# First norm of a two-layer DiT trunk: sums of squares on TensorE tile by tile, the first two adaLN tiles moved ahead, and a one-operation first guess of the root

## The chip, the cores and the metric

One core of a Trainium2 chip runs the whole program. The metric is device microseconds of that core, from the first to the last instruction and what lies around them; lower is better. Five engines work beside each other: TensorE (PE: matmuls, and PEld: its weight loads), VectorE (DVE), ScalarE (ACT), GpSimd (POOL) and SyncE (SP, which here issues most transfers).

## The reference, cut to what matters

Two layers of a backbone; what the change touches is the very first norm, and every reciprocal root in the program. D is 1024, the 256 latent and 256 context tokens are handled together as 512 columns.

```python
def rmsnorm(x, g):
    xf = x.astype(jnp.float32)
    y = xf * lax.rsqrt(jnp.mean(xf * xf, axis=-1, keepdims=True) + EPS)
    return y.astype(x.dtype) * g

mod_x = jnp.split((jax.nn.silu(c) @ p['w_ada'] + p['b_ada'])[:, None, :], 6, axis=-1)   # shift, scale, ...
hx = modulate(rmsnorm(xs, p['norm1_g']), mod_x[0], mod_x[1])     # h * (1 + scale) + shift
u = hx @ p['w_in']                                               # then four mixers, a merge, a SwiGLU
```

## The kernel before

Activations lie with channels on the 128 partitions and tokens along the free axis, so x is eight tiles `xs[k]` of 128 channels by 512 tokens. A product is taken as three matmuls on halves of a split operand (`mm3`: high by high, high by low, low by high). Weights arrive in chunks of eight 128-column blocks (`w_load`, a transfer by SP into `raw`) and are split by `w_ensure` into `whi` (a cast on ACT) and `wlo` (two subtractions on DVE).

The program starts with one serial stage, and then a loop over the eight tiles of channels:

- **Sums of squares.** `sq_add` squares each x tile on ACT as it lands and adds it on DVE into an accumulator, so that two tiles are left. `rstd_of(..., False)` calls `tok_sums` (line 469), which multiplies them by a column of ones: for each block of 128 tokens and each of the two tiles one matmul whose stationary side is the 128 by 128 piece of squares and whose moving side is one column. These are 8 matmuls; in float32 each runs as two passes, and the trace shows 16 pairs of weight load and matmul.
- **The root.** `rsqrt` (line 461) takes an integer first guess in two DVE operations (a shift into `rs_i`, then a multiply and add into `rs_y`) and improves it in seven more, each on 128 by 4 numbers, each waiting for the one before. The function serves all 17 roots of the program.
- **The broadcast.** `bcast` puts the root on all partitions with four PE transposes.
- **adaLN of one tile of channels.** `first_mod(u)` multiplies the conditioning vector by the columns of the modulation weights of tile u (16 small matmuls `mx<-u,cs`, 32 passes in the trace), copies the result on ACT, turns it with one matmul by `halves` (`mx<-cons,u`, 128x4), and makes shift and scale on DVE (`mod`, `moda`). Its weights are four transfers of 256 KB, put into SP's queue by `first_load(u)`.
- **The loop.** For each tile u, `norm_apply` makes the modulated tile in both halves (DVE `u<-u,moda,mx`, ACT, DVE), `first_mod(u + 1)` is called, and then 18 matmuls of 512 columns go into six accumulators (`pre`), followed by `first_load(u + 3)`.

Each engine works its own instructions in order. Their order is set by a scheduler that goes by dependences and by priorities from the place in the code, and `tc.high_priority()` lifts the root and the modulation's last operations.

Of the kernel before, what the change touches and what calls it, by code (L numbers as in the profile page):

```python
# [13 lines left out]
I32 = mybir.dt.int32  # L14
AF = mybir.ActivationFunctionType
ALU = mybir.AluOpType
AX = mybir.AxisListType

D = 1024
KD = D // 128  # L20
SEQ = 256
T = 512
L = 2
GRID_W = 64
EPS = 1e-6
# [115 lines left out]
def trunk(ctx: ExitStack, tc: tile.TileContext, xin: bass.AP, cin: bass.AP, par: bass.AP, con: bass.AP,  # L141
# [47 lines left out]
    U = Slots(upool, NSLOT)  # L189
# [4 lines left out]
    def nm(s):  # L194
        cnt[0] += 1
        return f"{s}_{cnt[0]}"
# [4 lines left out]
    def mx():  # L201
        return psx.tile([128, 512], F32, tag="mx", name=nm("mx"))

    def sm(shape, tag, dtype=F32, bufs=2):
        return small.tile(shape, dtype, tag=tag, name=nm(tag), bufs=bufs)

    def width(o):
        n_ = 1
        for d_ in o.shape[1:]:
            n_ *= d_  # L210
        return n_

    def stt(o, i0, s, i1, op0, op1):
        clk["dve"] += 65 + 1.17 * width(o)
        V.scalar_tensor_tensor(out=o, in0=i0, scalar=s, in1=i1, op0=op0, op1=op1)  # L215

    def tt(o, i0, i1, op):
        clk["dve"] += 65 + 1.1 * width(o)
        V.tensor_tensor(out=o, in0=i0, in1=i1, op=op)  # L219

    def red(o, i, op):
        clk["dve"] += 65 + 1.15 * width(i)
        V.tensor_reduce(out=o, in_=i, axis=AX.X, op=op)

    def ts(o, i0, s1, op0, s2=None, op1=None):
        clk["dve"] += 65 + 0.8 * width(o)
        if op1 is None:
            V.tensor_scalar(out=o, in0=i0, scalar1=s1, scalar2=None, op0=op0)
        else:
            V.tensor_scalar(out=o, in0=i0, scalar1=s1, scalar2=s2, op0=op0, op1=op1)  # L230

    MUL, ADD, SUB, MAX = ALU.mult, ALU.add, ALU.subtract, ALU.max
# [58 lines left out]
    xs = []  # L291
    for k in range(KD):
        t = U([128, T])
# [14 lines left out]
    for l in range(L):  # L308
        t = cpool.tile([128, NPAR], F32, name=f"par{l}")
# [3 lines left out]
    one = cpool.tile([128, 1], F32, name="one")  # L313
# [146 lines left out]

    def rsqrt(v, shape):

        y, s, ti = sm(shape, "rs_y"), sm(shape, "rs_s"), sm(shape, "rs_i", I32)
        with tc.high_priority():
            ts(ti, v.bitcast(I32), 1, ALU.logical_shift_right)
            ts(y.bitcast(I32), ti, -1, MUL, 0x5F3759DF, ADD)

            tt(s, y, y, MUL)
            tt(s, s, v, MUL)
            stt(s, s, -10.0 / 3, s, ADD, MUL)  # L470
            stt(y, s, 5.0, y, ADD, MUL)
            stt(s, y, -0.5 * 0.375 ** 3, y, MUL, MUL)
            tt(s, s, v, MUL)
            stt(y, s, 1.5 * 0.375, y, ADD, MUL)
        return y
# [12 lines left out]
    def rstd_of(sums, N, n, merge=True):  # L488
        shape = [128, len(sums), N // 128]
        if merge:  # L490
            r = sm(shape, "toks")
            for i, tiles in enumerate(sums):
                if len(tiles) == 2:
                    t = tiles.pop()
                    tt(tiles[0][:, :N], tiles[0][:, :N], t[:, :N], ADD)
                    U.put(t)
                p = mx()
                for b in range(N // 128):
                    PE.transpose(p[:, b * 128:(b + 1) * 128], tiles[0][:, b * 128:(b + 1) * 128], ident)
                red(r[:, i, :], p[:, :N].rearrange("p (b t) -> p b t", t=128), ADD)  # L500
            ts(r, r, 1.0 / n, MUL, EPS, ADD)
            return rsqrt(r, shape)
        r = sm(shape, "toks")
        ts(r, tok_sums(sums, N), 1.0 / n, MUL, EPS, ADD)
        return rsqrt(r, shape)

    def bcast(r, N):

        p = mx()
        for b in range(N // 128):  # L510
            PE.transpose(p[:, b * 128:(b + 1) * 128], r[:, b:b + 1].to_broadcast([128, 128]), ident)
        return p

    def sq_add(acc, src, N):

        t = U([128, N])
        A.activation(t[:, :N], src, AF.Square)
        acc = acc or []
        if len(acc) < 2:
            return acc + [t]  # L520
        tt(acc[0][:, :N], acc[0][:, :N], acc[1][:, :N], ADD)
        U.put(acc[1])
        return [acc[0], t]
# [71 lines left out]
    def first_load(u):  # L595
        if u < KD:
            ada_tiles[u] = [U([128, 512]) for _ in range(4)]
            for i_, t_ in enumerate(ada_tiles[u]):
                nc.sync.dma_start(t_, wfirst[u, i_])
# [3 lines left out]
    def first_mod(u):  # L603

        p = mx()
        for k in range(KD):
            for h in range(2):
                j = h + 2 * (k % 2)
                PE.matmul(p[32 * j:32 * j + 32, 0:128], cs[:, k, :],
                          ada_tiles[u][k // 2][:, (2 * (k % 2) + h) * 128:(2 * (k % 2) + h + 1) * 128], start=k < 2,  # L610
                          stop=k >= KD - 2, tile_position=(0, 32 * j), skip_group_check=True)
        U.put(ada_tiles.pop(u))
        sb = U([128, 128])
        A.copy(sb, p[:, 0:128])
        PE.matmul(p[:, 128:132], sb, halves, start=True, stop=True, skip_group_check=True)
        U.put(sb)
        o = PCOL["bada"][0]
        with tc.high_priority():
            tt(mods[0][:, u:u + 9:8, :], p[:, 128:132].rearrange("p (h s) -> p h s", h=2),
               params[0][:, o + u:o + u + 9:8].unsqueeze(2).to_broadcast([128, 2, 2]), ADD)  # L620
            stt(moda[:, u, :], mods[0][:, 8 + u, :], 1.0,
                params[0][:, PCOL["n1g"][0] + u:PCOL["n1g"][0] + u + 1].to_broadcast([128, 2]), ADD, MUL)
# [3 lines left out]
    first_load(1)  # L626
    w_load(1)
    first_load(2)
    nc.sync.dma_start(cons[:, nfirst:], con[:, nfirst:nres])
    acc = None  # L630
    for k in range(KD):
        acc = sq_add(acc, xs[k], T)
    rs = rstd_of([acc], T, D, False)
    U.put(acc)
    rb = bcast(rs[:, 0, :], T)
    hx = [None] * KD
    pre = [mm() for _ in range(4)] + [mx() for _ in range(2)]
    pos = w_take([(("w_in", 0), k, cols) for k in range(KD)
                  for cols in [misc_cols] + [ar(OFF["xbc"] + 128 * c) for c in FIRST]])
    W["ahead"], W["load"] = 0, 1  # L640
    began = clk["pe"]
    first_mod(0)
    for u in range(KD):
        hx[u] = U.pair(T)
        for s in range(2):
            norm_apply(hx, xs, s, rb, (moda, mods[0][:, 0:8, :]), u, s * SEQ)
        if u + 1 < KD:
            first_mod(u + 1)
        for i, ps in enumerate(pre):
            wh, wl = w_block(pos + 6 * u + i)  # L650
            mm3(ps, wh, wl, hx[u][0], hx[u][1], u == 0, u == KD - 1)
        first_load(u + 3)
    W["ahead"], W["load"] = AHEAD, NLOAD
    U.put(xs)
    for c0 in range(2048, 6144, 1024):
# [2 lines left out]
    for l in range(L):  # L658
# [643 lines left out]
        xs = []  # L1302
        for k in range(KD):
            t = U([128, N])
# [39 lines left out]
        for a, b in grp:  # L1344
# [28 lines left out]
            else:  # L1373
# [3 lines left out]
                r = out_by_stream(("w_ffn_out", l), act, b - a, a, 40, None if last else (l + 1, "n1g", 0))  # L1377
            U.put(act)
        if last:
            acc = r  # L1380
# [7 lines left out]
    rs = rstd_of([acc], SEQ, D, False)  # L1388
# [3 lines left out]
    for b in range(2):  # L1392
        for h in range(2):
            p, y = mm(), U([128, 512])
# [132 lines left out]
```

## Time and profile before

| | us |
|---|---|
| median of 3 runs | 1694.93 (1694.31 to 1698.3) |
| the profiled execution, as timed | 1695.51 |
| its span, first to last instruction | 1693.8 |
| PE busy in the span | 1649.6 (97%) |
| first 512-column matmul of the loop starts at | 24.84 |
| PE busy ahead of that, of 24.84 | 8.95 |

The page of the profile gives busy times, a row of 40 slices of the span and the chain of work that ended last. The timeline gives instructions in order of time, equal ones merged: start, time taken (of a merged row from its first start to its last end), engine, line, operation, and in brackets the engine's idle time before it and what ended that. PE's matmuls overlap, so how fast a stream of them goes is read from start to start and not from one matmul's own time.

### The profile page before, as it was taken

The page shows a single profiled execution, that of the slowest core. Times are in us where ns is not written, and L with a number is a line of the kernel's source. Part 1 is how long each engine was busy: PE and PEld are TensorE (multiplying, and loading weights), DVE is VectorE, ACT ScalarE, POOL GpSimd, SP SyncE. Part 2 cuts the span into 40 slices and gives each one's busy share as a digit, 9 for nine tenths or more (in the row PEclk, how much of TensorE's full clock was granted, in tenths as well). Part 3 has the DMA queues.
Part 4 walks back from the last instruction along what each step waited for, and adds up shares of the span by engine and source line. Part 5 has one row for each costly group of instructions (what it writes and reads, how often), then busy time and mean ns, then how long its engine had stood idle before and what let it go on. Part 6 is the DMA issues. An engine that isn't in the chain of part 4 may idle for free.

```text
span 1693.8 us, 26526 instructions
## 1 busy us (share of the span) xinstructions
PE 1649.6 (97%) x10078; PEld 1419.7 (84%) x10078; DVE 1296.1 (77%) x2644; ACT 799.4 (47%) x1350; POOL 52.6 (3%) x89
## 2 busy tenths in 40 slices
PE   6999999999999999999999999999999999999998
PEld 4777766778878888988888889978778999989998
DVE  4779999988578567887656657699899957876655
ACT  3475759462234234522212235457578445444444
POOL 0010200000000000000000000001111000000000
PEclk9999999999999999999999999999999999999999
DMA  9343321214435445355455646445432367645554
GB/s 365 112 142 120 114 69 54 75 38 137 152 126 183 138 148 190 132 189 174 149 168 200 219 150 196 144 130 166 123 104 94 114 223 231 207 151 185 184 180 147
DMA packets 85104, 259.18 MB, mean 153 GB/s; under 512 B 9648, under 2 KB 18784, under 8 KB 84976
## 3 DMA queue, kind: packets, MB, share of 16 engines
q1 hardware_dynamic: 73584, 244.15, 43.2%
q10 hardware_dynamic: 10624, 12.28, 2.9%
q8 instruction: 79, 1.29, 0.3%
q0 software_dynamic: 768, 1.05, 0.3%
q14 instruction: 49, 0.40, 0.1%
HBM read 253.70 MB, written 2.18 MB: 151 GB/s over the span
## 4 chain that ended last, share of the span: by engine, by line
PE 86%; ACT 4%; DVE 4%; DMA 4%; issue 1%; ACTq 0%; POOL 0%; DVEq 0%; SPq 0%
PE mm L176 76%; PE mx L176 9%; DMA u<-drow 3%; ACT u L152 2%; PE mx L180 2%; DVE u L215 1%; DVE wlo L219 1%; ACT whi L157 1%; ACT u L157 1%; DVE u L219 1%; DMA raw<-w_ada 0%; DVE u L230 0%; DMA u<-xin 0%; DMA c_raw<-cin 0%; DMA drow<-u 0%
## 5 line engine op out<-in xcount | busy, mean ns | idle before, releaser
L176 PE MATMUL mm<-u,whi 128*128 128x256 f32 (+1 forms) x5464 | 1300.5, 331 | 2.4 <-ACT u L152 2.1
L176 PEld LDWEIGHTS mm<-u,whi 128*128 128x128 f32 x5464 | 924.6, 190 | 103.8 <-issue 10.8
L176 PE MATMUL mm<-u,wlo 128*128 128x256 f32 (+1 forms) x2732 | 900.0, 330 | 0.0
L157 ACT CAST whi<-raw 128x1024 fp32r<-128x1024 f32 x351 | 367.8, 1048 | 557.8 <-PE mm L176 344.6
L219 DVE TENSOR_TENSOR wlo<-raw,whi 128x512 fp32r<-128x512 f32 x702 | 458.4, 689 | 185.5 <-ACT whi L157 183.2
L176 PEld LDWEIGHTS mm<-u,wlo 128*128 128x128 f32 x2732 | 520.0, 190 | 47.4 <-issue 2.7
L215 DVE SCALAR_TENSOR_TENSOR u<-raw,cs,u 128x512 f32<-128x512 f32 x210 | 148.3, 747 | 75.2 <-DMA raw<-w_ada 75.1
L152 ACT ACTIVATE u<-u 128x256 f32<-128x256 f32 (+6 forms) x248 | 116.5, 486 | 135.2 <-DVE u L219 85.3
L219 DVE TENSOR_TENSOR u<-u,u 128x256 f32<-128x256 f32 (+5 forms) x280 | 152.7, 564 | 9.0 <-ACT u L152 3.6
L176 PE MATMUL mx<-u,u 128*64 128x256 f32 (+6 forms) x644 | 128.3, 389 | 11.2 <-ACT whi L157 3.4
L215 DVE SCALAR_TENSOR_TENSOR u<-u,convw,u 128x510 f32<-128x510 f32 (+29 forms) x240 | 133.9, 601 | 0.0
L176 PEld LDWEIGHTS mx<-u,u 128*64 128x64 f32 (+3 forms) x644 | 77.8, 162 | 51.8 <-issue 12.8
L152 ACT ACTIVATE u<-mm 128x512 f32<-128x512 f32 (+3 forms) x148 | 71.8, 486 | 69.5 <-PE mm L176 65.0
L215 DVE SCALAR_TENSOR_TENSOR u<-u,mm 128x512 f32<-128x512 f32 (+1 forms) x132 | 72.4, 550 | 26.5 <-PE mm L176 24.9
L215 DVE SCALAR_TENSOR_TENSOR u<-u,u 128x512 fp32r<-128x512 f32 (+3 forms) x99 | 55.0, 570 | 10.3 <-ACT u L152 10.3
L157 ACT COPY u<-mx 128x512 f32<-128x512 f32 (+4 forms) x82 | 38.6, 498 | 39.3 <-PE mx L176 37.6
L176 PE MATMUL mm<-whi,u 128*128 128x512 f32 x160 | 51.5, 395 | 0.5 <-ACT u L152 0.5
L215 DVE SCALAR_TENSOR_TENSOR u<-u,par,u 128x510 f32<-128x510 f32 (+5 forms) x68 | 48.0, 714 | 0.2
L180 PE MATMUL mx<-cons,u 128*128 128x128 f32 (+1 forms) x276 | 41.4, 274 | 3.0 <-DVE u L219 1.2
L965 POOL TENSOR_SCALAR_AFFINE_SELECT u<-u 128x256 f32<-128x256 f32 x24 | 13.6, 565 | 987.0 <-DVE u L230 827.8
L180 PEld LDWEIGHTS mx<-cons,u 128*128 128x128 f32 (+1 forms) x276 | 31.7, 140 | 13.1 <-ACT u L152 4.0
L215 DVE SCALAR_TENSOR_TENSOR u<-mm,mod,u 128x256 f32<-128x256 f32 x64 | 30.1, 480 | 13.6 <-PE mm L176 13.4
(115 smaller groups left out, 805.9 us busy)
## 6 DMA issues: line engine op xcount, KB each, us to landing
raw<-wst SPq DMA_DIRECT2D x354, 512.0 KB, 3.3
raw<-w_ada SPq DMA_DIRECT2D x72, 512.0 KB, 4.1
u<-wfirst SPq DMA_DIRECT2D x32, 256.0 KB, 6.5
u<-drow ACTq DMA_DIRECT2D x32, 256.0 KB, 5.2
u<-xin SPq DMA_DIRECT2D x16, 256.0 KB, 4.1
u<-w_ada SPq DMA_DIRECT2D x16, 256.0 KB, 4.8
u<-drow ACTq DMA_DIRECT2D x16, 128.0 KB, 4.1
spill<-u SPq DMA_DIRECT2D x8, 128.0 KB, 3.1
```

Of the source, the lines that this page charges most:

```text
L152: nc.scalar.activation(o, *a, **k)
L157: nc.scalar.copy(o, i)
L176: PE._place(nc.tensor.matmul(*a, **k))
L180: PE._place(nc.tensor.transpose(*a, **k))
L215: V.scalar_tensor_tensor(out=o, in0=i0, scalar=s, in1=i1, op0=op0, op1=op1)
L219: V.tensor_tensor(out=o, in0=i0, in1=i1, op=op)
L965: G.affine_select(out=a_[:, 0:4:3], in_=a_[:, 0:4:3], pattern=[[0, 2], [1, 128]], compare_op=ALU.is_ge, fill=-1e5, base=0, channel_multipl ...
```

## The change

Four edits in the stage described above. The squares no longer pass DVE: each squared tile goes to PE as soon as ACT has it, and all eight tiles are summed there in one accumulator, 4 matmuls for each tile. `first_mod(0)` is called ahead of the root and `first_mod(1)` ahead of the loop; in the loop `first_mod(u + 2)` stands behind the 18 matmuls of tile u. The fourth group of modulation weights (`first_load(3)`) goes into SP's queue ahead of the rest of the constants, and the loop loads tile u + 4. And the root's first guess is one operation instead of two, in all 17 roots.

```diff
     def rsqrt(v, shape):
-        y, s, ti = sm(shape, "rs_y"), sm(shape, "rs_s"), sm(shape, "rs_i", I32)
+        y, s = sm(shape, "rs_y"), sm(shape, "rs_s")
         with tc.high_priority():
-            ts(ti, v.bitcast(I32), 1, ALU.logical_shift_right)
-            ts(y.bitcast(I32), ti, -1, MUL, 0x5F3759DF, ADD)
+            ts(y.bitcast(I32), v.bitcast(I32), -0.5, MUL, 0x5F3759DF, ADD)
...
     first_load(2)
+    first_load(3)
     nc.sync.dma_start(cons[:, nfirst:], con[:, nfirst:nres])
-    acc = None
+    p, r = mx(), sm([128, 4], "toks")
     for k in range(KD):
-        acc = sq_add(acc, xs[k], T)
-    rs = rstd_of([acc], T, D, False)
-    U.put(acc)
-    rb = bcast(rs[:, 0, :], T)
+        t = U([128, T])
+        A.activation(t, xs[k], AF.Square)
+        for b in range(4):
+            PE.matmul(p[:, b:b + 1], t[:, b * 128:(b + 1) * 128], one, start=k + b == 0, stop=k == KD - 1,
+                      skip_group_check=True)
+        U.put(t)
+    first_mod(0)
+    ts(r, p[:, 0:4], 1.0 / D, MUL, EPS, ADD)
+    rb = bcast(rsqrt(r, [128, 4]), T)
+    first_mod(1)
...
-    first_mod(0)
     for u in range(KD):
...
-        if u + 1 < KD:
-            first_mod(u + 1)
         for i, ps in enumerate(pre):
...
-        first_load(u + 3)
+        if u + 2 < KD:
+            first_mod(u + 2)
+        first_load(u + 4)
```

PE's order around the first broadcast (`mx<-one` are sums, `L180` the broadcast, `mx<-u,cs` the modulation), before:

```order
L176 MATMUL mx_170<-one,u_147 128x1
L176 MATMUL mx_170<-one,u_166 128x1
L180 MATMUL mx_192<-cons,rs_y_180 128x128 x4
L176 MATMUL mx_203<-u_118,cs 32x128 x4
L176 MATMUL mx_203<-u_119,cs 32x128 x4
L176 MATMUL mx_203<-u_120,cs 32x128 x4
L176 MATMUL mx_203<-u_121,cs 32x128 x4
L176 MATMUL mx_235<-u_128,cs 32x128 x4
L176 MATMUL mx_203<-cons,u_220 128x4
```

The last two of the eight rows of sums, and what follows, now:

```order
L176 MATMUL mx_155<-one,u_193 128x1 x4
L176 MATMUL mx_155<-one,u_199 128x1 x4
L176 MATMUL mx_205<-u_118,cs 32x128 x4
L176 MATMUL mx_205<-u_119,cs 32x128 x4
L180 MATMUL mx_238<-cons,rs_y_228 128x128
L176 MATMUL mx_205<-u_120,cs 32x128 x4
L180 MATMUL mx_238<-cons,rs_y_228 128x128 x3
L176 MATMUL mx_205<-u_121,cs 32x128 x4
L176 MATMUL mx_205<-cons,u_222 128x4
```

The sums went from 8 matmuls to 32; half of the first tile's modulation stands ahead of the broadcast and half is cut into it.

PE's order at the loop's first 512-column matmuls, before:

```order
L176 MATMUL mx_235<-u_130,cs 32x128 x4
L176 MATMUL mx_235<-u_131,cs 32x128 x4
L176 MATMUL mm_197<-u_225,whi_257 128x512
L176 MATMUL mx_235<-cons,u_252 128x4
L176 MATMUL mm_198<-u_225,whi_257 128x512
L176 MATMUL mm_199<-u_225,whi_257 128x512
L176 MATMUL mm_197<-u_226,whi_257 128x512
```

And now:

```order
L176 MATMUL mx_243<-u_129,cs 32x128 x4
L176 MATMUL mm_265<-u_271,whi_281 128x512
L176 MATMUL mm_266<-u_271,whi_281 128x512
L176 MATMUL mm_267<-u_271,whi_281 128x512
L176 MATMUL mx_243<-u_130,cs 32x128 x4
L176 MATMUL mm_268<-u_271,whi_281 128x512
L176 MATMUL mx_269<-u_271,whi_281 128x512
L176 MATMUL mx_243<-u_131,cs 32x128 x4
L176 MATMUL mm_265<-u_272,whi_281 128x512
L176 MATMUL mm_265<-u_271,wlo_282 128x512
L176 MATMUL mx_243<-cons,u_260 128x4
```

Half of the second tile's modulation moved from ahead of these matmuls into them. In the whole loop 6 groups of modulation matmuls stood among the 512-column ones before, and 10 stand there now; twice the turn by `halves` now follows its group at once, where one or two 512-column matmuls stood between them in every round before.

DVE's order from the root to the first tile's norm, before:

```order
L230 TENSOR_SCALAR toks_169<-mx_170 128x4
L228 TENSOR_SCALAR rs_i_182<-toks_169 128x4
L230 TENSOR_SCALAR rs_y_180<-rs_i_182 128x4
...
L215 SCALAR_TENSOR_TENSOR rs_y_180<-rs_s_181,rs_y_180 128x4
L219 TENSOR_TENSOR wlo_258<-raw_126,whi_257 128x512
L219 TENSOR_TENSOR mod_115<-mx_203,par_99 128x2x2
L219 TENSOR_TENSOR wlo_258<-raw_126,whi_257 128x512
L215 SCALAR_TENSOR_TENSOR moda_117<-mod_115,par_99 128x2
L215 SCALAR_TENSOR_TENSOR u_227<-u_79,moda_117,mx_192 128x256
```

And now:

```order
L230 TENSOR_SCALAR toks_156<-mx_155 128x4
L230 TENSOR_SCALAR rs_y_228<-toks_156 128x4
...
L215 SCALAR_TENSOR_TENSOR rs_y_228<-rs_s_229,rs_y_228 128x4
L219 TENSOR_TENSOR mod_115<-mx_205,par_99 128x2x2
L215 SCALAR_TENSOR_TENSOR moda_117<-mod_115,par_99 128x2
L215 SCALAR_TENSOR_TENSOR u_273<-u_79,moda_117,mx_238 128x256
L215 SCALAR_TENSOR_TENSOR u_277<-u_79,moda_117,mx_238 128x256
L219 TENSOR_TENSOR wlo_282<-raw_126,whi_281 128x512 x2
```

The shift into `rs_i` is gone, and the split of the first weights moved from between the modulation's operations to behind the first tile's norm. Further on the orders differ too: from the mixers of the first layer to the second layer's attention, PE, DVE and ACT have pieces in another order.

## Rows read from the trace of the kernel before

**Rows 1.** The page: busy time of each engine, and PE's busy tenths in 40 slices.

```profile
PE 1649.6 (97%) x10078; PEld 1419.7 (84%) x10078; DVE 1296.1 (77%) x2644; ACT 799.4 (47%) x1350; POOL 52.6 (3%) x89
PE   6999999999999999999999999999999999999998
```

**Rows 2.** Timeline, squares, last addition and sums (start, time taken, engine, operation).

```profile
4.23 1.20 ACT L152 ACTIVATE u<-u 128x512 f32<-128x512 f32 x2
...
9.75 1.19 ACT L152 ACTIVATE u<-u 128x512 f32<-128x512 f32 x2
...
12.08 0.69 DVE L219 TENSOR_TENSOR u<-u,u 128x512 f32<-128x512 f32 x1
...
12.88 3.49 PEld L176 LDWEIGHTS mx<-one,u 128*128 128x128 f32 x16 [12.88 <-issue]
```

**Rows 3.** Timeline, the root, one group of weight transfers, broadcast, modulation matmuls behind it.

```profile
16.50 0.16 DVE L230 TENSOR_SCALAR toks<-mx 128x4 f32<-128x4 f32 x1 [3.73 <-PE mx L176]
...
16.70 0.17 DVE L228 TENSOR_SCALAR rs_i<-toks 128x4 int32<-128x4 int32 x1
...
17.25 2.96 SPq L599 DMA_DIRECT2D u<-wfirst  x4
...
18.50 1.12 PE L180 MATMUL mx<-cons,rs_y 128*128 128x128 f32 x4 [2.04 <-DVE rs_y L215]
...
19.55 2.36 PE L176 MATMUL mx<-u,cs 128*32 128x128 f32 x40
```

**Rows 4.** Timeline, first weights' cast, and from the modulation's copy to the first 512-column matmul.

```profile
15.26 1.04 ACT L157 CAST whi<-raw 128x1024 fp32r<-128x1024 f32 x1 [4.31 <-DMA raw<-wst]
...
21.55 0.27 ACT L157 COPY u<-mx 128x128 f32<-128x128 f32 x1 [5.25 <-PE mx L176]
...
22.49 0.16 DVE L219 TENSOR_TENSOR mod<-mx,par 128x4 f32<-128x4 f32 x1 [3.44 <-PE mx L176]
...
23.17 0.16 DVE L215 SCALAR_TENSOR_TENSOR moda<-mod,par 128x2 f32<-128x2 f32 x1
23.36 0.87 DVE L215 SCALAR_TENSOR_TENSOR u<-u,moda,mx 128x256 f32<-128x256 f32 x2
...
24.84 0.79 PE L176 MATMUL mm<-u,whi 128*128 128x512 f32 x1 [0.94 <-ACT u L152]
```

**Rows 5.** Timeline of PE alone, 512-column matmuls in the loop's first round.

```profile
27.99 0.63 PE L176 MATMUL mm<-u,wlo 128*128 128x512 f32 x1
28.41 0.63 PE L176 MATMUL mm<-u,whi 128*128 128x512 f32 x1
...
31.23 0.40 PE L176 MATMUL mx<-u,wlo 128*128 128x512 f32 x1
```

**Rows 6.** Timeline of PE alone, one round of the loop and the next one's start.

```profile
37.78 1.08 PE L176 MATMUL mx<-u,cs 128*32 128x128 f32 x32
38.79 0.73 PE L176 MATMUL mm<-u,whi 128*128 128x512 f32 x2
39.36 0.28 PE L176 MATMUL mx<-cons,u 128*128 128x4 f32 x2
...
40.28 0.40 PE L176 MATMUL mm<-u,wlo 128*128 128x512 f32 x1
...
42.33 0.39 PE L176 MATMUL mx<-u,wlo 128*128 128x512 f32 x1
...
43.33 1.08 PE L176 MATMUL mx<-u,cs 128*32 128x128 f32 x32
44.34 0.73 PE L176 MATMUL mm<-u,whi 128*128 128x512 f32 x2
```

**Rows 7.** What PE waited for from 100 us on (total us, times, longest).

```profile
PE mx L180 <- DVE rs_y L215: 4.3, 5, 1.5
```

**Rows 8.** Timeline near the end: six sums, and what follows the last root.

```profile
1684.86 0.83 PE L176 MATMUL mx<-one,u 128*128 128x1 f32 x6
...
1687.75 1.27 ACT L152 ACTIVATE u<-mm,rs_y 128x512 f32<-128x512 f32 x2 [2.41 <-DVE rs_y L215]
```

## The prediction

> **What bounds the kernel now.** I read the page first: PE is busy 97% of the span, every slice but the first and the last is a 9 or close to it [rows 1]. So a microsecond is won only where PE stands still or where its own work shrinks, and the first slice, a 6, is the place the change is in. There I read the timeline. ACT squares the first two x tiles from 4.23, the last two until 10.94; DVE's last addition ends at 12.77; PE's sums start at 12.88 [rows 2]. From the sums a serial chain runs: root (16.50 to 18.50), broadcast, 32 modulation matmuls, copy (21.55), modulation, norm of tile 0, and the first 512-column matmul at 24.84 [rows 3, 4]. From there on the loop keeps PE busy without a gap, so whatever the first matmul gains or loses reaches the end of the loop, plus what the loop itself gains or loses.
>
> Two speeds stand in this stage. 512-column matmuls start 0.427 us apart at 28 us (512 columns at 1.2 GHz) and each takes 0.63; from 31.0 on each takes 0.40 [rows 5], and nine later ones go 0.228 apart (40.28 to 42.33) [rows 6]. So TensorE runs at its lower level until 31.0, after 6.2 us of the loop, and at 2.4 GHz afterwards; the page's clock row only says 9, so starts are what tells.
>
> **The change, part by part.** The sum goes against the profiled execution (span 1693.8, timed 1695.51, 0.6 above the median of 1694.93); differences are then put on the median.
>
> *Sums.* Before, 16 passes took 3.49 us [rows 2], 0.215 us from one to the next: a 128-column weight load for a single moving column, so the load is the price. The change has four times as many, 64. They start when the first square is done: 4.23 + 0.62, plus the 0.1 us that before lay between DVE's end and PE's start, so 4.95. Squares come every 0.6 to 1.7 us, and four tiles' worth of work is 1.7 us, so PE falls behind from the second tile on and never waits again. toks began 3.62 us after the first of 16 passes [rows 2, 3]; 48 more passes at 0.215 make 10.3. So toks starts at 4.95 + 3.62 + 10.3 = 18.9 where it started at 16.50: **2.4 us later**, though DVE's six additions are gone and the start is 8 us earlier. The other end of this price: at the upper level the six sums near the end start 0.11 us apart (0.83 for six, less the last one's own 0.25) [rows 8]; that is a rival below.
>
> *Root.* One operation less, 0.20 us from start to start (16.50 to 16.70) [rows 3]. toks to broadcast was 2.0, now 1.8: broadcast at 20.7 where it was at 18.50.
>
> *Modulation of tile 0.* Broadcast to copy took 3.05 us (18.50 to 21.55) [rows 3, 4], with 32 passes behind the broadcast at about 0.055 (40 in 2.36) [rows 3]. Now 16 stand ahead of the broadcast and run while DVE makes the root: 0.88 saved. The other 16 are queued behind PE's wait for the root, though their data is there, and are cut into the transposes: two more changes of form, 0.2 each (19.55 less the broadcast's four starts at 0.21 each). So 2.6, and the copy at 23.3. ACT's cast of the first weights, done at 16.3 before [rows 4], now stands behind that copy; its 1.04 us is covered by `mod`, `moda` and DVE's first product (1.3 us plus 0.5), and would cost up to 1 us uncovered. On DVE the split no longer stands between `mod` and `moda`: 23.17 becomes 22.69 by the usual 0.20 step, so copy to product is 1.33 and not 1.81 [rows 4]. Product at 24.6, first matmul 1.48 later: 26.1. Against 24.84 that is **+1.2**.
>
> *Loop.* Half of tile 1's modulation, 16 passes, ran in PE's idle time before and now lies among the matmuls: 16 × 0.055 = **+0.9**. Groups of such matmuls among the 512-column ones go from 6 to 10. One round before took 5.55 (38.79 to 44.34) [rows 6]; 18 matmuls at 0.228 are 4.10, 32 passes at 0.027 (half of 0.055) 0.87, the two `halves` passes 0.22; the 0.36 that is left is one change of form there and back. Four more: **+1.4**, and if the first two groups, at the lower level, cost double, 0.7 on top. Twice `halves` follows its group at once and waits for ACT's copy; before, two matmuls (0.46) filled that wait (38.79 to 39.36 holds them) [rows 6]. I take 0.4 each, **+0.8**; bounds 0 and 0.9.
>
> *The other roots.* Of 17, five held PE after 100 us (4.3 us in all) [rows 7], and the last holds ACT at the end [rows 8]. At 0.20 each, 6 × 0.20 = **−1.2**; bounds −0.2 (only the last) and −2.4 (twice the step, where DVE has other work between the root's).
>
> *Transfers.* The moved group of weights stands ahead of the constants and the third weight chunk in SP's queue; SP issues one such group in 3.0 us [rows 3], so those come 3 us later. The chunk is wanted in the third round, the constants behind the loop, so nothing; with that cover gone it would be those 3.0.
>
> *Order further on.* Not visible in the trace of before; a single wait of the listed kind is 1.5 us at most [rows 7], so a regrouping may give or take a few of them: 0, with ±3 for the range.
>
> Sum: 1.2 + 0.9 + 1.4 + 0.8 − 1.2 = **+3.1**, on the median 1698.
>
> **A rule against the row.** The row: 3.5 us of back-to-back sums stayed at 0.215 a pass, and the clock rose only in the loop [rows 2, 5]. The Trainium skill, "TensorE: Matmul & The Clock Gate", section "What's actually happening", says that the array's slow clock is the default and that sustained activity releases it; by that rule the 13.9 us stream of sums would raise it, and the time would be that of the first rival. The same page, "Part 4: PE-mode transpose", says that transposes do not count as busy in the way that matmuls do; by that a stream of weight loads with one column each may count as little. No run here yet shows which.
>
> **The rivals.**
>
> *One: the clock rises during the sums (faster).* For it: they are now an unbroken stream on PE for 13.9 us, four times as long as before. Against it: each pass moves one column, and what went before the rise at 31.0 was 512-column work [rows 5]. Price: rise near 10 us; 24 passes done, 40 left at 0.11 make 4.4, toks at 14.6; broadcast 16.4; the rest of the tile's modulation at half its price 1.4, copy 17.8, product 19.1, first matmul 20.6: −4.2. The 14 matmuls that ran at the lower level (6.2 us at 0.427) save 0.2 each: −2.8. The loop's terms are 0.45 + 1.4 + 0.8, the roots −1.2. Sum −5.55: **1689**.
>
> *Two: the clock rises later in the loop (slower).* Before, the rise came 6.2 us after the first 512-column matmul, of which the last 5 held nothing else [rows 5]. Now the first round is cut by modulation groups and by a `halves` that waits. Every microsecond of delay costs 1 − 0.228/0.427 = 0.47 us. My sum already lets the rise move along by 1.2, to 32.2; slower than before by over 0.3% (5.1 us, about what a measurement can tell from no change) needs 2.0 us more, 4.3 us of delay, a rise after 36.5. A rise at 40 makes 7.8 × 0.47 = 3.7, in all +6.8: **1702**.
>
> *Three: the later orders decide.* The mixers' pieces fall otherwise and give or take several waits. Each of the PE waits is small [rows 7]; it would take four of them. Either sign, 1692 or 1704.
>
> *Four: it does what it says.* The norm is reached sooner, PE keeping up with the squares. By rows this needs a pass under 0.15 us (0.6 us a tile over 8 passes is less still), so it is rival one or nothing.
>
> **How the numbers follow.** Forecast (clock low through the sums) 0.50; rival one 0.32; two 0.11; three 0.07, half each way. Faster by over 0.3%: rival one lands at −5.55 ± 3.5 (the three of the order, and where the rise falls), so 0.6 of it, and half of three: 0.22. Slower: most of two (0.08), half of three (0.03), and a seventh of the forecast's own spread (3.1 ± 2, 0.07): 0.18. Within: 0.60. The range takes the forecast's bounds (1693 to 1702) and reaches down to the greater part of rival one: 1687 to 1702.
>
> **What would show it.** Right: the sums' 64 passes start 0.215 us apart from about 4.95 and end near 18.8; toks near 18.9, broadcast near 20.7, first 512-column matmul near 26; the rounds after the third 5.5 to 6.0 long; 17 DVE operations fewer by `rs_i`. Wrong: sums at 0.11 apart or toks before 16.5 (rival one); matmuls 0.427 apart beyond 36 (rival two); a first matmul before 24.8 with sums at 0.215 would mean my chain is mis-sized; a loop no longer than before would refute the changes of form.

## The result, and the profile after

The kernel after takes 1707.76 us (median of 4 runs, 1706.0 to 1710.31) where the kernel before took 1694.62 beside it (4 runs): a ratio of 1.0076, 95% interval 1.0054 to 1.0098, or **13 us slower**. The forecast was 1698, the range 1687 to 1702. The profiled execution has a span of 1708.6, against 1693.8.

The page after, PE's busy time and its tenths in 40 slices, to be held against [rows 1]:

```profile
PE 1670.1 (98%) x10126; PEld 1434.8 (84%) x10126; DVE 1290.1 (76%) x2621; ACT 799.7 (47%) x1350; POOL 55.8 (3%) x89
PE   8999799999999999999999999999999999999998
```

PE is *more* busy than before, by 20.5 us, with 48 passes more (the sums). Two digits tell where to look: the first slice went from 6 to 8 and the fifth (171 to 214 us) from 9 to 7. A rising busy time is not work well done here: at the lower level of the clock a 512-column matmul takes 0.427 us from start to start in place of 0.228 [rows 5, 6], and counts as busy all that time.

The head, PE's timeline after (columns as in [rows 2]), answering to [rows 2 to 4]:

```profile
5.08 13.78 PE L176 MATMUL mx<-one,u 128*128 128x1 f32 x64 [5.08 <-ACT u L152]
18.79 1.08 PE L176 MATMUL mx<-u,cs 128*32 128x128 f32 x16
20.70 0.48 PE L180 MATMUL mx<-cons,rs_y 128*128 128x128 f32 x1 [0.83 <-DVE rs_y L215]
...
26.07 1.65 PE L176 MATMUL mm<-u,whi 128*128 128x512 f32 x3 [0.89 <-ACT u L152]
```

64 passes in 13.78 us are 0.215 each, all at the price of before; the broadcast starts at 20.70 and the first 512-column matmul at 26.07. The forecast had 20.7 and 26.1. So the head costs 1.2 us, as worked out. The other 13.6 us of the span come later. They are found by following one thing that both kernels do in the same order: the casts of weights on ACT (`whi<-raw`, 351 in all). Their starts:

| | before | after | difference |
|---|---|---|---|
| first 512-column matmul | 24.84 | 26.07 | +1.2 |
| 9th cast (the loop's end) | 69.5 | 76.3 | +6.8 |
| 25th cast | 174.7 | 181.0 | +6.4 |
| 37th cast (first layer's mixers over) | 303.0 | 317.9 | +14.9 |
| 351st cast (near the end) | 1681.5 | 1696.6 | +15.0 |

Two places, then: 5.6 us in the loop and 8.5 us in the first layer's mixers. Nothing that lasts comes after that.

The seventh of the loop's eight rounds, PE's timeline after:

```profile
64.83 0.38 PE L176 MATMUL mx<-cons,u 128*128 128x4 f32 x2 [0.39 <-ACT u L157]
66.40 1.41 PE L176 MATMUL mm<-u,whi 128*128 128x512 f32 x4 [1.18 <-ACT u L152]
67.61 0.63 PE L176 MATMUL mm<-u,wlo 128*128 128x512 f32 x1
68.04 0.63 PE L176 MATMUL mm<-u,whi 128*128 128x512 f32 x1
...
70.60 0.41 PE L176 MATMUL mm<-u,wlo 128*128 128x512 f32 x1
```

No round of the kernel before had such a wait [rows 6]. The turn of the last modulation waits for ACT's copy (0.39), then PE waits 1.18 for the norm of this round's tile. DVE's timeline after says why:

```profile
63.49 1.29 DVE L219 TENSOR_TENSOR wlo<-raw,whi 128x512 fp32r<-128x512 f32 x2
65.25 0.16 DVE L219 TENSOR_TENSOR mod<-mx,par 128x4 f32<-128x4 f32 x1 [0.47 <-PE mx L176]
65.33 0.47 DVE L215 SCALAR_TENSOR_TENSOR u<-u,moda,mx 128x256 f32<-128x256 f32 x1
```

`mod` of the last tile stands ahead of the norm's product, and has to wait for PE's turn by `halves`; the product that PE in its turn waits for comes behind it. Then the matmuls start 0.427 apart until 70.60: TensorE is at 1.2 GHz again for about 3 us, which for 7 matmuls at 0.427 instead of 0.228 costs 1.4.

The first layer's mixers: busy time of each engine from 180 to 220 us (length, then busy time and count of PE, PEld, DVE, ACT, POOL, then granted clock, DMA share, GB/s), before:

```profile
180.00:220.00 40.00, 38.51 (x188) 27.79 (x187) 37.81 (x78) 26.72 (x57) 7.54 (x12) 1.00 0.36 105
```

and after:

```profile
180.00:220.00 40.00, 30.90 (x129) 19.28 (x128) 34.34 (x74) 23.80 (x55) 11.57 (x14) 0.79 0.30 79
```

PE's idle time goes from 1.5 to 9.1 us and the granted clock from 1.00 to 0.79; with two levels that is 2 × 0.21 × 40 = 17 us at the lower one. A third fewer matmuls are run. Which ones are missing is seen in the timeline, PE before (rows of 512-column matmuls between the products `mx<-u,u` left out):

```profile
181.04 0.65 PE L176 MATMUL mx<-u,u 128*64 128x256 f32 x2
...
184.11 1.08 PE L176 MATMUL mx<-u,u 128*64 128x256 f32 x8
...
188.33 1.94 PE L176 MATMUL mx<-u,u 128*64 128x256 f32 x14
```

and after:

```profile
187.37 0.65 PE L176 MATMUL mx<-u,u 128*64 128x256 f32 x2 [0.87 <-DVE u L219]
191.10 1.97 PE L176 MATMUL mx<-u,u 128*64 128x256 f32 x8 [3.08 <-DVE u L219]
193.00 0.80 PE L176 MATMUL mm<-whi,u 128*128 128x512 f32 x1
193.73 1.98 PE L176 MATMUL mx<-u,u 128*64 128x256 f32 x8
...
204.49 1.22 PE L176 MATMUL mm<-u,whi 128*128 128x512 f32 x2 [2.74 <-ACT u L157]
...
208.89 0.66 PE L180 MATMUL mx<-cons,u 128*128 128x128 f32 x2 [1.47 <-DVE u L219]
```

Before, 10 to 13 matmuls of 512 columns stand between the small products and PE does not wait there at all; after, none or one, at most seven, stand there and PE waits 3.08, 2.74 and 1.47. In the list of waits of the kernel after (total, times, longest) the first two of these stand in the first line and the sixth; the root's waits, the subject of [rows 7], are 4.1 in all and 1.1 at most, no longer what counts:

```profile
PE mx L176 <- DVE u L219: 6.1, 5, 3.1
...
PE mm L176 <- ACT u L157: 2.7, 1, 2.7
```

### The profile page after: what moved, and what is told of

The parts are those of the page before. It is cut to its first block, busy times and chain, and to the rows that moved or that the text cites. A ratio compares the mean times of both kernels' runs of the same rounds, so it can differ in the third digit from the quotient of the medians.

```text
span 1708.6 us, 26588 instructions
## 1 busy us (share of the span) xinstructions
PE 1670.1 (98%) x10126; PEld 1434.8 (84%) x10126; DVE 1290.1 (76%) x2621; ACT 799.7 (47%) x1350; POOL 55.8 (3%) x89
## 4 chain that ended last, share of the span: by engine, by line
PE 91%; DVE 3%; DMA 3%; ACT 2%; issue 1%; POOL 0%; ACTq 0%; DVEq 0%; SPq 0%
PE mm L176 78%; PE mx L176 10%; PE mx L180 2%; DMA u<-drow 2%; DVE wlo L219 1%; DVE u L215 1%; ACT whi L157 1%; ACT u L152 1%; DVE u L219 1%; DVE u L230 0%; ACT u L157 0%; DMA u<-u 0%; DMA raw<-w_ada 0%; DMA c_raw<-cin 0%; DVE rs_s L219 0%
## 5 line engine op out<-in xcount | busy, mean ns | idle before, releaser
L215 DVE SCALAR_TENSOR_TENSOR u<-raw,cs,u 128x512 f32<-128x512 f32 x210 | 148.3, 746 | 76.3 <-DMA raw<-w_ada 76.2
L219 DVE TENSOR_TENSOR u<-u,u 128x512 f32<-128x512 f32 (+5 forms) x274 | 149.1, 563 | 9.0 <-ACT u L152 4.4
L152 ACT ACTIVATE u<-mm 128x256 f32<-128x256 f32 (+3 forms) x148 | 71.8, 487 | 67.2 <-PE mm L176 61.7
L215 DVE SCALAR_TENSOR_TENSOR u<-u,u 128x256 fp32r<-128x256 f32 (+3 forms) x99 | 55.1, 569 | 11.4 <-ACT u L152 11.3
L971 POOL TENSOR_SCALAR_AFFINE_SELECT u<-u 128x256 f32<-128x256 f32 x24 | 20.1, 839 | 993.4 <-DVE u L230 854.1
L180 PE MATMUL mx<-cons,u 128*128 128x128 f32 (+1 forms) x276 | 40.9, 276 | 2.0 <-DVE u L219 1.5
L180 PEld LDWEIGHTS mx<-cons,u 128*128 128x128 f32 (+1 forms) x276 | 32.0, 142 | 11.7 <-issue 4.6
```

The costliest lines, as they stand in the source:

```text
L152: nc.scalar.activation(o, *a, **k)
L180: PE._place(nc.tensor.transpose(*a, **k))
L971: G.affine_select(out=a_[:, 0:4:3], in_=a_[:, 0:4:3], pattern=[[0, 2], [1, 128]], compare_op=ALU.is_ge, fill=-1e5, base=0, channel_multipl ...
```

## The experiments

Each kernel was timed beside the kernel before. The casts below are those of the table above; "first matmul" is the first one of 512 columns.

| kernel | ratio to before, 95% interval | first matmul | 9th cast | 25th | 37th |
|---|---|---|---|---|---|
| after | 1.0076 (1.0054 to 1.0098) | 26.07 | 76.3 | 181.0 | 317.9 |
| e1_root | 1.0035 (1.0022 to 1.0049) | 25.05 | 70.0 | 174.3 | 310.0 |
| e2_sums | 1.0021 (1.0006 to 1.0036) | 26.63 | 74.9 | 178.4 | 308.1 |
| e3_mods | 1.0036 (1.0022 to 1.005) | 23.19 | 72.9 | 176.8 | 304.3 |
| e4_head | 1.0026 (1.0012 to 1.004) | 25.46 | 75.7 | 179.8 | 307.4 |
| f4_acct | 1.0037 (1.0023 to 1.0051) | 24.88 | 69.5 | 174.6 | 308.6 |
| f2_rootclk | 1.0006 (0.9996 to 1.0016) | 25.80 | 67.6 | 172.7 | 304.5 |
| f3_afterclk | 1.0036 (1.0023 to 1.0049) | 25.95 | 78.8 | 182.2 | 312.0 |
| h4_f3load | 1.0020 (1.0009 to 1.0032) | 25.85 | 76.5 | 180.1 | 311.2 |
| h3_whole | 0.9986 (0.9977 to 0.9996) | 24.73 | 68.2 | 172.6 | 301.6 |
| g4_two | 0.9990 (0.9980 to 0.9999) | 22.32 | 66.1 | 170.7 | 300.1 |

**The edits one at a time.** Four kernels, three with one edit alone and one with all but the root.

The root alone (e1_root), in the kernel before:

```diff
-            ts(ti, v.bitcast(I32), 1, ALU.logical_shift_right)
-            ts(y.bitcast(I32), ti, -1, MUL, 0x5F3759DF, ADD)
+            ts(y.bitcast(I32), v.bitcast(I32), -0.5, MUL, 0x5F3759DF, ADD)
```

> Only the root's first guess in one operation; sums, modulation and loop as before. Its instruction order in the first layer's mixers is nearly the changed kernel's. Order theory (the first-layer loss of the changed kernel comes from the order that the shorter root brings): first 512-column matmul 0.2 us earlier than before (24.6), loop end as before, then about +8 us between 180 and 320 us, in all +6 to +8 (1701 to 1703). Head theory (the loss is carried over from the sums, the modulation or the moved transfers): no such loss, the roots' 0.2 us each stay a gain, 1693 to 1694.

Measured: 1702.1, slower. The loop is as before, the first matmul 0.2 later (expected 0.2 earlier); between the 25th and the 37th cast it goes from -0.3 to +7.0. An operation was taken out, the head was left alone, and the loss in the mixers stands there in full.

The sums alone (e2_sums):

```diff
-        acc = sq_add(acc, xs[k], T)
+        t = U([128, T])
+        A.activation(t, xs[k], AF.Square)
+        for b in range(4):
+            PE.matmul(p[:, b:b + 1], t[:, b * 128:(b + 1) * 128], one, ...)
```

> Only the sums of squares tile by tile on TensorE (64 passes); two-operation root, modulation calls and transfers where they were. Both theories: passes 0.215 us apart from 5.0 to 18.8, toks 18.9, first 512-column matmul near 27 (+2.2), 15 groups of modulation matmuls inside the loop's matmuls instead of 6, at 0.36 each +3.2, and 0.9 for half a tile's modulation: +6 by the end of the loop. Order theory: it stays near that (1700 to 1702, the first layer's mixers stand in the order of before). Head theory: the loss between 180 and 320 us is there too, 1708.

Measured: 1700.13. First matmul +1.8, 9th cast +5.3, and nothing of the mixers' loss (37th +5.1). The loop loses 3.5 although no line of it was edited: its modulation groups came out split.

The modulation and its transfers alone (e3_mods):

```diff
+    first_load(3)
...
+    first_mod(0)
     rs = rstd_of([acc], T, D, False)
     rb = bcast(rs[:, 0, :], T)
+    first_mod(1)
...
-        if u + 1 < KD:
-            first_mod(u + 1)
...
-        first_load(u + 3)
+        if u + 2 < KD:
+            first_mod(u + 2)
+        first_load(u + 4)
```

> Only the modulation moved ahead (first two tiles, then two tiles ahead in the loop) with its transfers; sums on VectorE and two-operation root as before. First 512-column matmul earlier, near 22.5 (-2.3), since the first tile's modulation runs while the root is made. The loop has the changed kernel's order, with the norm of the last but one tile split around the last modulation: +5.6 there. Order theory: mixers in the order of before, nothing further: +3.3 in all, 1698. Head theory with the moved transfers as cause: the loss between 180 and 320 us is there, 1706.

Measured: 1702.07. First matmul 1.6 earlier, 9th cast 3.4 later: the loop itself takes 5.0 more. At the 37th cast it is +1.3; the rest comes between the 193rd and the 217th cast (1099 to 1222 us), where more matmuls run at the lower level (+4.7 at the end). The order theory's 1698 was missed, the loss in the mixers is not there.

All but the root (e4_head), the kernel after with the two lines of the guess put back:

> The changed kernel with the two-operation root put back: sums, modulation and transfers as changed. First 512-column matmul near 26.3, loop end +7. Order theory: no further loss in the first layer's mixers, +7 in all, 1701 to 1702. Head theory: as the changed kernel, 1708.

Measured: 1700.47. First matmul +0.6, 9th cast +6.1, 37th +4.3: the loop's loss without the mixers'. So the mixers' loss comes with the root's edit and the loop's with the rest. The traces bear it out: from the loop's last rounds to the end, PE, DVE and ACT run e4_head in the order of the kernel before, and e1_root in that of the kernel after, instruction by instruction.

**Why a shorter root makes the mixers slower.** Not in the trace but in the code: the order of the mixers is made by a planner, `interleave` (line 560), which decides at each step whether a piece of the linear work (`lin`, the 512-column matmuls) or of a mixer comes next, and goes by an account of each engine's time:

```python
        clk["dve"] += 65 + 0.8 * width(o)      # in ts(), for each operation
...
            if len(can) > 1 and w == 0 and max(clk["dve"], mixed) + lookahead < clk["pe"]:
                w = min(can[1:], key=lambda w_: steps[w_])
```

An operation less in a root lowers DVE's account by 65 + 0.8 × width, 68 for four numbers. Each root lowers the sum that is compared once more, until the condition can turn and a mixer's piece is taken where a piece of `lin` was, or the reverse; from there the orders part. At which step it turns stands in no trace, but that the account does it can be tried: two kernels separate the account from the instructions.

f4_acct keeps every instruction of the kernel before and changes the account alone:

```diff
             ts(y.bitcast(I32), ti, -1, MUL, 0x5F3759DF, ADD)
+            clk["dve"] -= 65 + 0.8 * width(y)
```

> The kernel before, with every instruction of the root kept; only the planner's account of DVE is lowered by the price of one operation for each root (65 + 0.8 x width), as leaving out the operation lowers it. Theory P (the account): in the first layer the planner's choices flip as they did when only the root was changed, the SSM products stand back to back on PE again, the clock falls there; first 512-column matmul as before (24.8 +- 0.2), the ninth cast of the loop's weights +0, the thirty-seventh +7 (5 to 9), the end +6 to +11: ratio 1.004. Theory R (the shorter root itself, its times and not the order, costs): nothing is shorter here, so as before, ratio 0.999 to 1.001, thirty-seventh cast within 1.

Measured: 1701.86, slower by 6 us with not one instruction more or less. PE's order is that of the kernel before until 174.6 us, and the 9th and the 25th cast are those of before to 0.1; at the 37th it is +5.6. PE's timeline of f4_acct at the place:

```profile
183.86 1.33 PE L176 MATMUL mx<-u,u 128*64 128x256 f32 x8 [2.31 <-DVE u L219]
185.20 0.80 PE L176 MATMUL mm<-whi,u 128*128 128x512 f32 x1
185.92 1.98 PE L176 MATMUL mx<-u,u 128*64 128x256 f32 x8
...
196.57 1.22 PE L176 MATMUL mm<-u,whi 128*128 128x512 f32 x2 [3.15 <-ACT u L157]
```

The products stand together, and the waits are of the size of those in the kernel after. From 180 to 220 the granted clock is 0.83 and PE idles 7.7 us:

```profile
180.00:220.00 40.00, 32.29 (x138) 21.11 (x137) 36.15 (x78) 22.16 (x50) 7.94 (x12) 0.83 0.22 67
```

f2_rootclk is the reverse: the one-operation guess, with the account kept as it was (`clk["dve"] += 65 + 0.8 * width(y)` behind it).

> The kernel before with the root's first guess in one operation, and the planner's account of DVE kept as if there were still two: the change of the root alone, the order of the mixers as before. Theory P: the thirty-seventh cast within 1 of before, no fall of the granted clock between 180 and 330; the end -0.2 to -2.4 (6 roots at 0.20 that something waits for make -1.2), ratio 0.9993 (0.9985 to 1.000). Theory R: the thirty-seventh cast +5 to +7 as when only the root was changed, ratio 1.0035.

Measured: 1696.48 against 1695.97, no difference that can be measured. But for some pieces (on PE near 150, from 169 to 202, near 226 us and in the second layer) the orders are those of before, and the 7 us are gone: the theory of the account holds. e1_root runs the same instructions, on PE in the same order until 174 us, and has the loss. But two points of the expectation missed. The gain of the shorter roots is not in the time, though PE's waits for them went from 6.3 to 5.3 us in all; and the 37th cast is +1.4 after -2.0 at the 25th, because the clock fell at one wait. That wait is worth a look, since it stands in the kernel before too. PE's timeline before:

```profile
247.44 2.85 PE L176 MATMUL mx<-u,u 96*128 96x512 f32 x8 [1.58 <-ACT u L152]
```

and of f2_rootclk:

```profile
246.60 5.49 PE L176 MATMUL mx<-u,u 96*128 96x512 f32 x8 [1.58 <-ACT u L152]
```

The same row, the same 1.58 us of waiting, and the eight products take 2.85 us in the one and 5.49 in the other. To see whether that belongs to the kernel or to the execution, both programs were profiled once more.

> The same program as the one with the root alone and the account kept, profiled a second time. If the clock's fall at 246.6 (6.8 us, the thirty-seventh cast from -2 to +1.4) and its early rise at 26 belong to the kernel, both stand there again. If they belong to the execution (the same 1.58 us wait stands in the kernel before without a fall), one or both are missing, the ninth cast is between -2 and +1 and the thirty-seventh equals it to 1 us.

> The kernel before, profiled a second time. Theory E (when the clock rises and falls differs from one execution to the next): order, waits and starts as in the first profile relative to one another, but the rise in the first 512-column matmuls not at 31.0, or a stretch at half clock somewhere else than 1205; span within 4 of 1693.8. Theory K (rise and fall follow from the kernel's own work): the rise 6.2 after the first 512-column matmul, one fall near 1205 of 3.4 and none at 247.

Measured, f2_look:

```profile
244.50 4.54 PE L176 MATMUL mx<-u,u 96*128 96x512 f32 x8 [1.58 <-ACT u L152]
```

The fall is there again, if shorter (4.54 for the eight), and so is an early rise of the clock in the head. In before_look the first rise comes 6.2 us after the first matmul and there is no fall at that place, both as in the first profile, but there are falls at 1134 and 1496 that the first did not have. From 1485 to 1520, before and then before_look:

```profile
1485.00:1520.00 35.00, 33.38 (x303) 30.64 (x302) 25.09 (x59) 16.38 (x28) 0.00 (x0) 1.00 0.44 147
```

```profile
1485.00:1520.00 35.00, 33.38 (x293) 30.79 (x292) 24.17 (x59) 16.07 (x27) 0.00 (x0) 0.95 0.41 136
```

One program, PE busy for the same 33.38 us, the clock 1.00 in one execution and 0.95 in the other. The two further falls account for 1.4 and 1.3 us of the 2.9 by which its span is longer (its casts go from +0.6 to +2.0 at the first and from +1.7 to +3.0 at the second). So single falls are partly a matter of the execution, and a difference of 3 us between two profiles says little; that of f2_rootclk at 246 came twice out of two. The order does not decide it: g4_two and h3_whole (below) have PE's order of f2_rootclk from 90 us on and the same 1.58 us of waiting, and their eight products take 2.85. In the traces of all kernels here this wait stands eleven times, five times with a fall behind it.

**The loop.** f3_afterclk is the kernel after with the account kept:

```diff
             ts(y.bitcast(I32), v.bitcast(I32), -0.5, MUL, 0x5F3759DF, ADD)
+            clk["dve"] += 65 + 0.8 * width(y)
```

> The kernel after, with the planner's account of DVE kept as if the root still had two operations. Theory P: head and loop as in the kernel after (first 512-column matmul 26.1, ninth cast +6 to +7), then no further loss to the thirty-seventh cast (+4 to +7 in place of +15), no clock below full between 180 and 330, the end +3 to +6: 1698, ratio 1.002 to 1.003. Theory R: as after, ratio 1.0076, the thirty-seventh cast +15.

Measured: 1701.88, ratio 1.0036. From the 9th cast (+9.3) to the 37th (+9.0) nothing is lost any more, so that the account carries 1.0076 - 1.0036 = 0.0040, 6.8 us, of the 13. The expectation missed in the head: the 9th cast is 2.5 later than in the kernel after, though the order up to there is the same, because the clock rose later (below); and one fall stands in the trace near 257, behind the same 1.58 us of waiting.

h4_f3load takes the early transfer out as well:

```diff
-    first_load(3)
...
-        first_load(u + 4)
+        first_load(u + 3)
```

> The kernel after without the early transfer (one group of modulation weights less ahead, each later one a round later, as before), the planner's account of DVE kept. Theory T (the early transfer lets the last modulation fall into the last round, whose norm then waits for it): the 1.18 us wait near 66 and the fall of the clock behind it are gone, 14 groups of modulation matmuls in the loop in place of 11 (three at 0.36: +1.1); ninth cast +4 to +6 where the kernel after had +6.8; ratio 1.002 to 1.003. Rival: the wait near 66 stays, since DVE's order sets it: ninth cast +7 or more.

Measured: 1699.95, ratio 1.0020. The 1.18 us wait and the fall behind it are gone: with the weights a round later, six 512-column matmuls of that round stand between the last group and its turn by `halves`. Its 9th cast is +7.0, more than expected: the clock rose at 34.9 here, as late as in f3_afterclk. Behind the wait of 1.58 us, at 253, the clock fell here too. The orders of the two programs show 15 groups of modulation matmuls in the loop, against 10 with the early transfer (the expectation had 14 and 11). The ratio falls by 0.0016 from f3_afterclk, but the intervals overlap: a gain of 2.7 us from this edit alone is likely and not shown.

h3_whole keeps the sums on PE, the one-operation root and the account, and gives the loop back its old form and transfers; both first modulations stand ahead of the broadcast:

```diff
-    rb = bcast(rsqrt(r, [128, 4]), T)
     first_mod(1)
+    rb = bcast(rsqrt(r, [128, 4]), T)
...
+        if 0 < u < KD - 1:
+            first_mod(u + 1)
...
-        if u + 2 < KD:
-            first_mod(u + 2)
```

> The kernel after with the loop's order and transfers of before (the third tile's modulation onwards ahead of each round's matmuls, no early transfer), the modulation of both first tiles ahead of the broadcast, and the planner's account of DVE kept: sums on PE as in the change, the groups of modulation matmuls whole. Worked from the run with the same order and DVE's sums (first 512-column matmul 22.32, its sums' end 16.3): sums end 18.8, first 512-column matmul 24.8 (24.3 to 25.3). Theory L (split groups, early transfer and the last round are what the loop lost): ninth cast within 2.5 of before (the clock's rise moves it by that much), no wait over 0.5 in the loop; ratio 0.999 to 1.0005. Rival S (the sums on PE and the squares on ACT delay the loop's casts themselves): ninth cast +4 to +6 as with PE's sums alone, ratio 1.002 to 1.003.

Measured: 1693.89 against 1696.42: 2.5 us *faster* than before, a ratio of 0.9986. PE's timeline of h3_whole:

```profile
4.97 13.78 PE L176 MATMUL mx<-one,u 128*128 128x1 f32 x64 [4.97 <-ACT u L152]
18.68 1.93 PE L176 MATMUL mx<-u,cs 128*32 128x128 f32 x32
...
22.11 1.12 PE L180 MATMUL mx<-cons,rs_y 128*128 128x128 f32 x4
...
24.73 0.79 PE L176 MATMUL mm<-u,whi 128*128 128x512 f32 x1
```

The modulation fills PE's wait for the root, the broadcast does not wait at all, and the loop has its 6 whole groups. That is theory L, a little better than its range; rival S is out. From h4_f3load to h3_whole the ratio falls by 0.0034, 5.8 us: this is what the split groups and the cut broadcast cost, together with a late rise of the clock. In the two profiles the rise came 9.1 and 2.0 us after the first matmul, and 7.1 us at the lower level make 3.3 (at 0.47 each, by the prediction's price); whether it comes late because the groups are split is not shown.

g4_two is the same with DVE's sums of before:

> The kernel before with DVE's sums of squares, the modulation of the first two tiles ahead of the broadcast (behind the token sums), the loop's order and the transfers' as before, the root's guess in one operation and the planner's account kept. The 16 passes and the product with halves fill PE's wait for the root. Theory H (the head's gain holds where the loop's groups stay whole): token sums from 12.9, broadcast at 18.3, first 512-column matmul at 21.4 to 22.4 (-2.4 to -3.4), ninth cast -2.5 to -3.5, the end -3 to -5 with the roots: 1691, ratio 0.9975. Rival W (the gain is taken back by weights that have not landed or been cast, or by the clock, which rises only after as much matmul work): first matmul as in H, but the ninth cast -1 or less, ratio 0.999 to 1.000. Rival O (any shift of the loop shuffles the mixers' waits by a few us): ratio 1.001 or more.

```profile
19.70 1.12 PE L180 MATMUL mx<-cons,rs_y 128*128 128x128 f32 x4
...
22.32 0.80 PE L176 MATMUL mm<-u,whi 128*128 128x512 f32 x1
```

First matmul 22.32 (2.5 us earlier than before, as theory H had it), 9th cast -3.4; 1693.87 against 1695.97, ratio 0.9990, where 0.9975 was expected. Up to the loop's end theory H holds, in the time it does not. The clock as rival W has it did not take the gain back: it rose 3.0 us after the first matmul, where it took 6.2 before. g4_two and h3_whole are the two that beat the kernel before, by about 2 us. The sums on PE put the first matmul 2.4 us later than DVE's (24.73 against 22.32), and of that the times of the two show nothing: the interval of either is as wide.

## Why the prediction was wrong

- **Sums, root, modulation: right.** Start 5.08 for 4.95, 0.215 a pass, broadcast 20.70 for 20.7, first matmul 26.07 for 26.1.
- **Rival one: refuted.** All 64 passes stayed at 0.215. The Trainium skill, "TensorE: Matmul & The Clock Gate", section "What's actually happening", lets sustained activity release the clock; 13.8 us of loads with one moving column each did not, in any of the six kernels with these sums. Whether what the Trainium skill says of transposes on that page ("Part 4: PE-mode transpose") covers such passes, no run here shows.
- **Rival two: not in the profile of after, and yet a real thing.** There the rise came at 29.66, earlier than before. In f3_afterclk and h4_f3load, with the same order of the head, it came at 35.1 and 34.9.
- **Loop: mis-sized.** 3.1 forecast, 5.6 measured. The 10 groups were counted rightly. The turn by `halves` without cover was there too, and waited 0.39 as forecast (0.4). What was missed is who waits behind it: DVE's `mod`, and behind that the norm of the round's own tile (1.18), and 1.4 at the lower level. Together 2.6. That this is about the difference is luck: the sum had the rise 6.2 us after the first matmul, it came after 3.6, and those 2.6 us gave 1.2 back, so that the loop itself lost 6.8. Of the 1.1 that is left, up to 0.7 is the double price of two groups at the lower level, which the prediction names and leaves out of its sum, and 0.25 a wait of PE for `mod`, at 45.78. e3_mods, whose clock rose 6.0 us after the first matmul and did not fall behind its wait of 1.19, loses 5.0 in the loop. The step on transfers is at fault too: it asked only whether weights moved back in the queue are still in time, and not what weights that come earlier do to the order.
- **Roots: -1.2 forecast.** PE's waits for roots did shrink by 1.0 us in f2_rootclk, but its time shows nothing of it.
- **Order further on: the step that failed.** It stood at 0 with ±3, from waits of 1.5 us at most. It was +8.5 in the trace. The ratios give 5 to 7 us for the account: 0.0040 from after to f3_afterclk, 0.0037 for f4_acct, 0.0029 from e1_root to f2_rootclk. Rival three named the mechanism, with 0.07 and four waits to the good or bad. Both sizes came from the waits of the kernel before, and those are small *because* the planner had put matmuls in front of each: once they are elsewhere, the wait is the whole of DVE's or ACT's step (2.3 to 3.2 us), and the clock fell behind it in all three traces that have these waits (after, e1_root, f4_acct), so that what runs next takes nearly twice as long (the eight products 1.97 in place of 1.08). Of the 8.5 us, PE's idle time from 180 to 330 explains 3.2 (9.2 against 6.0). The other 5.2 is busy time: between the 25th and the 37th cast PE runs 598 matmuls in both kernels, and is busy for 122.4 us before and for 127.6 after, of which 13.8 lie at the lower level.

The 13 us, put together from the ratios: the account 6.8, the split groups and the cut broadcast 5.8 (with the clock's late rise in it), the early transfer 2.7 (not shown by itself), and what is left of the change -2.4.

## What to carry to other kernels

Where a planner orders a kernel by its own account of engine times, every edit that changes the account is an edit of the order: lay the planned orders of before and after side by side at the places where PE waits for nothing, and hold the account fixed to time the edit itself. Price a wait that loses its cover by the whole step that it then waits for, with the chance that the matmuls behind it run at the lower clock, and not by the waits in the old profile. Small matmuls moved ahead pay where they fill a wait as one group; cut into a stream of large ones they cost more than they saved.

## What the runs showed of the hardware that was not expected

- **A wait of 1 to 3 us may halve the clock, or not.** The Trainium skill, "TensorE: Matmul & The Clock Gate", section "HAM oscillation — how this bites in real kernels", has pauses between matmul work throttle the clock again. In these runs pauses as short as 1.2 to 1.6 us were followed by a fall (66.40 in after, 246.60 in f2_rootclk), and the same pauses were not: 1.58 us in the kernel before, and 1.19 us in e3_mods, at the place where after, e4_head and f3_afterclk have 1.18 and a fall. What tells the two apart stays open. Each of the two falls that could be isolated (in before_look) cost 1.3 to 1.4 us.
- **When the clock first rises does not follow from the order alone.** With one order of the head it came 3.6 us after the first 512-column matmul (after, at 29.66) and 9.1 us (f3_afterclk, at 35.1). PE's timeline of after, where equal matmuls take 0.80 ahead of the step and 0.50 behind it:

```profile
28.23 0.80 PE L176 MATMUL mm<-u,whi 128*128 128x512 f32 x1
...
29.85 0.50 PE L176 MATMUL mm<-u,whi 128*128 128x512 f32 x1
```

And of f3_afterclk, where the step lies in the row of 34.71, whose second matmul starts at 35.13:

```profile
34.29 0.63 PE L176 MATMUL mx<-u,wlo 128*128 128x512 f32 x1
34.71 0.80 PE L176 MATMUL mx<-u,whi 128*128 128x512 f32 x2
35.35 0.39 PE L176 MATMUL mx<-u,wlo 128*128 128x512 f32 x1
```

That is worth up to 2.5 us at the loop's end (76.3 against 78.8), the size of what the whole stage had to give. The prediction's reading of [rows 5], that 512-column work goes ahead of the rise, does not hold in every run either: in both profiles of f2_rootclk (the second is f2_look), with PE's rows in the order of the kernel before, the rise came ahead of the first such matmul, at 24.7 and 23.4, while PE ran the modulation. That matmul, in f2_rootclk, takes 0.50 where it took 0.79 before [rows 4]:

```profile
25.80 0.50 PE L176 MATMUL mm<-u,whi 128*128 128x512 f32 x1 [0.94 <-ACT u L152]
```
